# Splitting each accumulator right behind its last merge, ahead of the next superblock's input columns

## The chip, the cores and the metric

The kernel runs on one core of one Trainium2 chip. A core has five engines that run side by side, each with its own list of instructions that it works through in the written order: TensorE (PE, matrix products into PSUM banks), VectorE (DVE), ScalarE (ACT), GpSimd (POOL) and SyncE (SP, which here only starts transfers). ACT starts transfers as well. Engines wait for each other through semaphores. The metric is the device time of one execution in microseconds (us); lower is better.

## The reference

One layer of a decoder with three branches in parallel, on 2048 tokens of 1024 channels:

```python
h = rms_norm(x, norm_g[l])
p = h @ w_in[l]                       # 1024 -> 7552, split into the branches' inputs
y_a = rwkv7_mix(...) * silu(z_a)      # delta-rule recurrence, 512 channels
y_b = sliding_window_sink_attn(...) * silu(z_b)
y_c = memory_cross_attn(...) * silu(z_c)
gates = sigmoid(p_gate).reshape(bsz, t, 3, 1024)
merged = (gates[:, :, 0] * (y_a @ w_proj_a[l]) + gates[:, :, 1] * (y_b @ w_proj_b[l])
          + gates[:, :, 2] * (y_c @ w_proj_c[l]))
x = x + merged @ w_out[l]
```

All inputs and outputs are float32.

## The kernel before

The tokens are worked through in four *superblocks* `sb` = 0 to 3 of 512 tokens. Activations lie transposed: channels on the 128 partitions, tokens along the row. Dense products keep float32 accuracy by splitting each operand into a high part (rounded to the format fp32r, a copy on ACT) and a low part (the rest, a subtraction on DVE); each product is then three matmuls, high by high, high by low and low by high, into one PSUM bank (`gemm3`, lines 430 to 432, and the same three in `output`, lines 1137 to 1139).

A weight is fetched by `wblock` as a 128x512 piece. In superblock 0 the raw piece is loaded by SP (line 411, tile `raw`, three buffers), its high part is made by ACT (line 412), its low part by DVE (line 413), and both are stored to DRAM by SP (line 416). The later superblocks load both parts ready made (line 408), with no work on ACT or DVE. The split pieces `whl` have eight buffers.

A superblock ends in a tail with these pieces:

- `merge(0, ...)`, the last of three merges into the eight accumulators `accs` (tiles `mB`, one for each block of 128 output channels, called block 0 to block 7 here). For each block PE runs 12 matmuls into a bank `mm` (two buffers), DVE multiplies the bank by the gate (line 1119, which frees the bank) and adds the product to the accumulator (line 1120). So PE can start block o only when line 1119 of block o - 2 is done.
- `x_cols(sb + 1, rb)`, the normalised input `hH`/`hL` of the next superblock: for each of eight column blocks a load of the transposed `x` on ACT's queue (line 1181), a multiplication on DVE (line 1182), the high part on ACT (line 1184) and the low part on DVE (line 1185). The last superblock has none.
- `output(sb, accs)`: first each accumulator is split into a high part (`a`, a tile `g2`, line 1126 on ACT) and a low part (`b`, a tile `mB`, line 1128 on DVE). There are nine `mB` buffers for eight accumulators, so a low part takes the buffer that the split before it freed. Then two halves n = 0, 1 of 512 output columns: for each block k a piece of `w_out`, and 12 matmuls into four banks (two `mm`, two `as_`), 192 in all. At the end of a half, `x` is loaded (ACT queue), added by DVE (line 1144, which frees the bank) and stored (ACT queue).

The order of the instructions on each engine isn't the order of the Python code. `order` collects all instructions, `lay_out` plays them through with estimated costs, and the resulting list of each engine is fixed. At each step it takes, among the instructions of an engine that are ready, the one with the lowest *rank*. The rank is the place in the program (line `s.rank = len(out)`), with a few corrections: readers of PSUM off PE, such as line 1119, come 600 places earlier, and weight pieces up to 1000 places earlier:

```python
        s.rank = len(out)
        if any(r[0].startswith("whl") and (s.bytes or r[5] == F32R) for r in s.writes):
            s.rank = max(s.rank - ahead, min(s.rank, 15))
        if s.eng != "PE" and any(r[4] for r in s.reads):
            s.rank -= 600
```

So moving code in the program moves ranks, and through them the lists.

Of the kernel before, what the change touches and what calls it, by code (L numbers as in the profile page):

```python
# [9 lines left out]
F32 = mybir.dt.float32  # L10
F32R = mybir.dt.float32r
BF16 = mybir.dt.bfloat16
I32 = mybir.dt.int32
AF = mybir.ActivationFunctionType
ALU = mybir.AluOpType
# [4 lines left out]
TB = 512  # L20
# [265 lines left out]
def build(tc, A, nsb=4):  # L286
    nc = tc.nc
    es = ExitStack()
    V, S, G, PE = nc.vector, nc.scalar, nc.gpsimd, nc.tensor

    def pool(name, bufs, **kw):
        return es.enter_context(tc.tile_pool(name=name, bufs=bufs, **kw))
# [7 lines left out]
    mp = pool("mp", 9)  # L300
# [5 lines left out]
    def g2(dt=F32, shape=(128, TB)):  # L306
        return gp_.tile(list(shape), dt, name="g2")
# [3 lines left out]
    def mm_ps():  # L311
        return ps.tile([128, 512], F32, name="mm", bufs=2)
# [4 lines left out]
    def s_ps():  # L317
        return ps.tile([128, 512], F32, name="as_", bufs=2)
# [41 lines left out]
    def pcol(name, i=0):  # L360
        o, w = PV[name]
        return pv[:, o + i:o + i + 1]
# [13 lines left out]
    def dcol(name, i=0):  # L376
        return dv[:, DV[name][0] + i:DV[name][0] + i + 1]
# [27 lines left out]
    def wblock(src, key=None):  # L405
        w = wp.tile([128, 2, 512], F32R, name="whl")
        if key in kept:
            nc.sync.dma_start(w.bitcast(F32), kept[key])
            return w[:, 0], w[:, 1]
        raw = wp.tile([128, 512], F32, name="raw", bufs=RAW)  # L410
        nc.sync.dma_start(raw, src)
        S.activation(w[:, 0], raw, AF.Copy)  # L412
        V.tensor_tensor(w[:, 1], raw, w[:, 0].bitcast(F32), op=ALU.subtract)  # L413
        if key is not None and nsb > 1:
            kept[key] = dp.tile([128, 2, 512], F32, name=f"k{len(kept)}")
            nc.sync.dma_start(kept[key], w.bitcast(F32))
        return w[:, 0], w[:, 1]
# [8 lines left out]
    def gemm3(out, pairs):  # L426

        n = len(pairs)
        for i, ((lh, ll), (rh, rl)) in enumerate(pairs):
            PE.matmul(out, lh, rh, start=i == 0, stop=False)  # L430
            PE.matmul(out, lh, rl, start=False, stop=False)  # L431
            PE.matmul(out, ll, rh, start=False, stop=i == n - 1)  # L432
# [30 lines left out]
    def proj(blk, hT, n=TB):  # L463
        o = mm_ps()
        gemm3(o[:, :n], [(w, (hT[0][:, k, :n], hT[1][:, k, :n])) for k, w in enumerate(wtiles(A["w_in"][blk], 8, ("in", blk)))])
        return o
# [166 lines left out]
    def shift(o, blk, mu, omu, sb, tag, bufs=1):  # L633
        t = rp.tile([128, TB], F32, name=tag, bufs=bufs)
        S.activation(t, o, AF.Copy, scale=omu)
        V.scalar_tensor_tensor(t[:, 1:], o[:, :TB - 1], mu, t[:, 1:], op0=ALU.mult, op1=ALU.add)
        V.scalar_tensor_tensor(t[:, 0:1], carry[sb % 2][:, blk:blk + 1], mu, t[:, 0:1], op0=ALU.mult, op1=ALU.add)
        V.tensor_copy(carry[1 - sb % 2][:, blk:blk + 1], o[:, TB - 1:TB])
        return t
# [461 lines left out]
    def gate(i, o, hT):  # L1101
        gp = proj(B_G + 8 * i + o, hT)
        t = gp_.tile([128, TB], F32, name="gt", bufs=2) if i else g2()
        S.activation(t, gp, AF.Tanh, scale=0.5)  # L1104
        return t

    def merge(i, yh, yl, accs, hT, first=False, orange=range(8), gates=None):
        for o in orange:
            yield 3.718
            w = [t.rearrange("p (k c) -> p k c", k=4) for t in wblock(A["w_proj"][i, o], ("proj", i, o))]  # L1110
            g = gates[o] if gates else gate(i, o, hT)
            pp = mm_ps()
            gemm3(pp, [((w[0][:, k], w[1][:, k]), (yh[k], yl[k])) for k in range(4)])
            if first:
                acc = mp.tile([128, TB], F32, name="mB")
                V.scalar_tensor_tensor(acc, g, 1.0, pp, op0=ALU.add, op1=ALU.mult)
                accs.append(acc)
            else:
                V.scalar_tensor_tensor(g, g, 1.0, pp, op0=ALU.add, op1=ALU.mult)  # L1119
                V.tensor_tensor(accs[o], accs[o], g, op=ALU.add)  # L1120

    def output(sb, accs):
        mh, ml = [], []
        for o in range(8):
            a = g2(F32R)
            S.activation(a, accs[o], AF.Copy)
            b = mp.tile([128, TB], F32R, name="mB")
            V.tensor_tensor(b, accs[o], a.bitcast(F32), op=ALU.subtract)
            mh.append(a)
            ml.append(b)  # L1130
        for n in range(2):
            op = [mm_ps(), s_ps(), mm_ps(), s_ps()]
            for k in range(8):
                wh, wl = wblock(A["w_out"][n, k], ("out", n, k))
                for tt in range(4):
                    tk = slice(tt * 128, (tt + 1) * 128)
                    PE.matmul(op[tt], mh[k][:, tk], wh, start=k == 0, stop=False)  # L1137
                    PE.matmul(op[tt], mh[k][:, tk], wl, start=False, stop=False)  # L1138
                    PE.matmul(op[tt], ml[k][:, tk], wh, start=False, stop=k == 7)  # L1139
            for tt in range(4):  # L1140
                rows = slice(sb * TB + tt * 128, sb * TB + (tt + 1) * 128)
                xr = g2()
                nc.scalar.dma_start(xr, A["x"][rows, n * 512:(n + 1) * 512])
                V.scalar_tensor_tensor(xr, op[tt], 0.5, xr, op0=ALU.mult, op1=ALU.add)
                nc.scalar.dma_start(A["out"][rows, n * 512:(n + 1) * 512], xr)
# [7 lines left out]
    def x_norm(sb):  # L1153
        t = hT_tiles()
        norm_T(4, pcols("norm_g"), *t, x0)
        return t
# [32 lines left out]
    hT = x_norm(0)  # L1189
# [3 lines left out]
    for sb in range(nsb):  # L1193
        wa = proj(B_WA, hT)
        low = shift(wa, B_WA, pcol("mu_wa"), dcol("omu_wa"), sb, "rr_")
        S.activation(low[EV], low[EV], AF.Tanh)

        lwla = [rp.tile([128, TB], F32R, name=f"lwla{i}") for i in range(2)]
        for t, h, o in zip(lwla, (EV, OD), (OD, EV)):
            S.activation(t[h], low[h], AF.Copy)  # L1200
            V.tensor_tensor(t[o], low[h], t[h].bitcast(F32), op=ALU.subtract)
        yas = []
        ya, yb, yc_ = ([], []), ([], []), ([], [])
        accs = []

        def stream_r():
            n = 2
            for p0 in range(0, 4, n):
                group, Z = [], rp.tile([128, 2, 2, NC_, C], F32, name="Z")
                dk = xp.tile([128, 2, NC_], F32, name="dk", bufs=2)  # L1210
                Nc = rp.tile([128, 2, NC_, 32], F32, name="Nc")
                for p in range(p0, p0 + n):
                    yield from rwkv_prep(p, p - p0, Z, dk, Nc, sb, hT, lwla, group)
                yield from rwkv_inverse(group, Z, Nc)
                yield from rwkv_chain(group, Z, dk, hT, yas)
            while pend:
                pend.pop(0)()
            yield 0.412

        def stream_f():  # L1220
            for h in range(4):
                yield from cross_head(h, sb, hT, *yc_)
            if not sb:
                rope_tables(0)
            yield from swa_kv(sb, hT)
            yield 6.938
            for j in range(4):
                yield from weave(swa_pair(j, sb, hT, *yb), merge(2, *yc_, accs, hT, first=True, orange=(2 * j, 2 * j + 1)))
            yield from merge(1, *yb, accs, hT)
            for o in range(8):  # L1230
                gates.append(gate(0, o, hT))
                yield 5.908

        gates = []
        for _ in weave(*(paced(g, PACE[min(sb, 1)][i]) for i, g in enumerate((stream_r(), stream_f())))):
            pass
        for p in range(4):
            split_y(yas[p], *ya, "a", p, sb)
        rb = None
        if sb + 1 < nsb:  # L1240
            rope_tables(sb + 1)
            rb = x_scales(sb + 1)
        for _ in merge(0, *ya, accs, hT, gates=gates):
            pass
        if rb is not None:
            hT = x_cols(sb + 1, rb)
        output(sb, accs)
    order(tc, manual)
    es.close()


def paced(g, paces):

    for f, d in zip(paces, g):
        yield f * d
# [85 lines left out]
```

## Time and profile before

| | us |
|---|---|
| median of the runs of before | 2281.17 (2280.58, 2281.17, 2286.04) |
| time of the profiled execution | 2283.99 |
| its span, first to last instruction | 2282.2 |
| PE busy | 2241.2 (98%) |
| DVE busy | 1541.3 (68%) |
| ACT busy | 916.9 (40%) |
| mean granted PE clock | 0.995 of full speed |

Of one execution the profile gives for each instruction when it started, how long it took, and, in square brackets, how long its engine had been idle just before and what ended that idle time. A row of the timeline reads: start in us from the span's beginning, duration, engine, line of the code, operation, output tile <- input tiles, shapes, how many were merged into the row. Matmuls overlap: one starts about every 0.23 us though each is shown as 0.39 us long, so gaps on PE are read from start to start. A share of busy time is a mean over stages that differ, and the change touches only the four tails, so they are looked at one by one.

### The profile page before, as it was taken

What the parts mean: (1) busy time and instruction counts of PE and PEld (TensorE: products, weight loads), DVE (VectorE), ACT (ScalarE), POOL (GpSimd) and SP (SyncE); (2) the same over time, 40 slices, a digit from 0 to 9 for tenths busy, and PEclk for the clock granted to TensorE, in tenths of its full rate; (3) what the DMA queues carried; (4) which work ended last, traced back from release to release, by engine and by line L of the source; (5) the groups of instructions that cost most, each with busy time, mean ns of one, the idle gap of its engine ahead of it and who ended that gap; (6) DMA issues with size and microseconds to landing.
All of it is one profiled execution on the core that took longest, in us unless ns stands there. A gap on an engine that the chain in (4) does not pass through costs nothing.

```text
span 2282.2 us, 36933 instructions
## 1 busy us (share of the span) xinstructions
PE 2241.2 (98%) x13684; PEld 1814.2 (79%) x13684; DVE 1541.3 (68%) x3967; ACT 916.9 (40%) x2006; POOL 148.6 (7%) x209
## 2 busy tenths in 40 slices
PE   7999989999999999999999999999999999999999
PEld 6788778777788877878888877877888887777887
DVE  6799689775568777954427967884345795796312
ACT  5554564545244354433214344442222535434210
POOL 2000010000000010000001001000000001000000
PEclk9999999999999999999999999999999999999999
DMA  6767546679844443437774434445675444343655
GB/s 215 273 225 252 185 153 217 222 258 341 302 155 160 146 148 130 157 138 239 232 265 129 151 127 139 157 136 183 231 252 196 155 147 151 115 153 121 204 193 193
DMA packets 146226, 430.55 MB, mean 189 GB/s; under 512 B 16640, under 2 KB 21120, under 8 KB 146048
## 3 DMA queue, kind: packets, MB, share of 16 engines
q1 hardware_dynamic: 129920, 398.83, 52.1%
q10 hardware_dynamic: 16128, 29.37, 3.9%
q8 instruction: 109, 1.79, 0.3%
q14 instruction: 69, 0.57, 0.1%
HBM read 333.24 MB, written 94.90 MB: 188 GB/s over the span
## 4 chain that ended last, share of the span: by engine, by line
PE 70%; DVE 12%; ACT 3%; DMA 2%; issue 1%; POOL 0%; SPq 0%; ACTq 0%; DVEq 0%; POOLq 0%
PE mm L431 17%; PE mm L430 17%; PE mm L432 16%; PE rw L731 1%; DVE ibc L779 1%; PE mm L1139 1%; PE mm L1137 1%; PE mm L1138 1%; PE rw L852 1%; PE oo L1092 1%; DVE ibc L780 1%; PE oo L967 1%; PE rw L845 1%; DVE Yi L781 1%; PE rw L837 1%
## 5 line engine op out<-in xcount | busy, mean ns | idle before, releaser
L430 PE MATMUL mm<-hH,whl 128*128 128x512 f32 x1888 | 751.1, 398 | 4.6 <-DVE g L899 3.8
L431 PE MATMUL mm<-hL,whl 128*128 128x512 f32 x1888 | 752.4, 398 | 0.0
L432 PE MATMUL mm<-hH,whl 128*128 128x512 f32 x1888 | 747.4, 396 | 0.0
L430 PEld LDWEIGHTS mm<-hH,whl 128*128 128x128 f32 x1888 | 355.7, 188 | 76.7 <-DVE g L899 4.3
L431 PEld LDWEIGHTS mm<-hL,whl 128*128 128x128 f32 x1888 | 355.6, 188 | 71.1 <-issue 0.7
L432 PEld LDWEIGHTS mm<-hH,whl 128*128 128x128 f32 x1888 | 355.8, 188 | 68.6
L412 ACT ACTIVATE whl<-raw 128x512 fp32r<-128x512 f32 x178 | 111.7, 630 | 183.4 <-PE mm L432 79.6
L413 DVE TENSOR_TENSOR whl<-raw,whl 128x512 fp32r<-128x512 f32 x178 | 123.6, 696 | 65.7 <-ACT whl L412 64.6
L430 PE MATMUL mm<-yh,whl 128*128 128x512 f32 x384 | 152.8, 398 | 1.4 <-DVE g L1119 1.4
L431 PE MATMUL mm<-yl,whl 128*128 128x512 f32 x384 | 151.4, 394 | 0.0
L432 PE MATMUL mm<-yh,whl 128*128 128x512 f32 x384 | 151.3, 394 | 0.0
L843 ACT ACTIVATE SP<-Z,Pl 64x64 f32<-64x64 f32 x256 | 88.3, 345 | 118.7 <-DVE Z L853 114.9
L779 DVE STREAM_SHUFFLE ibc<-Nc 128x496 f32<-128x496 f32 (+30 forms) x248 | 113.2, 474 | 0.1
L1119 DVE SCALAR_TENSOR_TENSOR g<-g,mm 128x512 f32<-128x512 f32 x32 | 21.9, 686 | 127.5 <-PE mm L432 127.4
L780 DVE TENSOR_TENSOR ibc<-ibc,Yi 128x496 f32<-128x496 f32 (+30 forms) x248 | 104.7, 422 | 3.5
L781 DVE TENSOR_TENSOR Yi<-Yi,ibc 128x496 f32<-128x496 f32 (+30 forms) x248 | 103.6, 418 | 1.2
L853 DVE SCALAR_TENSOR_TENSOR Z<-rw,Pl,SP 64x64 f32<-64x64 f32 x224 | 63.5, 283 | 46.6 <-PE rw L852 42.9
L1104 ACT ACTIVATE gt<-mm 128x512 f32<-128x512 f32 x64 | 37.8, 591 | 129.3 <-PE mm L432 129.2
L430 PEld LDWEIGHTS mm<-yh,whl 128*128 128x128 f32 x384 | 72.1, 188 | 16.6 <-DVE g L1119 2.5
L432 PEld LDWEIGHTS mm<-yh,whl 128*128 128x128 f32 x384 | 72.1, 188 | 14.8
L1066 ACT ACTIVATE g<-g,mxs,st 128x256 f32<-128x256 f32 (+1 forms) x128 | 74.6, 584 | 22.8 <-DVE mxs L1059 22.5
L431 PEld LDWEIGHTS mm<-yl,whl 128*128 128x128 f32 x384 | 72.2, 188 | 13.9
(1882 smaller groups left out, 3789.6 us busy)
## 6 DMA issues: line engine op xcount, KB each, us to landing
whl<-k SPq DMA_DIRECT2D x486, 512.0 KB, 3.3
k<-whl SPq DMA_DIRECT2D x162, 512.0 KB, 3.2
raw<-in_w_in SPq DMA_DIRECT2D x118, 256.0 KB, 3.7
g<-in_x ACTq DMA_DIRECT2D x32, 256.0 KB, 5.0
out<-g ACTq DMA_DIRECT2D x32, 256.0 KB, 3.6
raw<-in_w_proj SPq DMA_DIRECT2D x24, 256.0 KB, 3.6
rt<-in_x ACTq DMA_DIRECT2D x24, 256.0 KB, 5.2
rt<-in_xt ACTq DMA_DIRECT2D x24, 256.0 KB, 5.5
```

The costliest lines, as they stand in the source:

```text
L412: S.activation(w[:, 0], raw, AF.Copy)
L413: V.tensor_tensor(w[:, 1], raw, w[:, 0].bitcast(F32), op=ALU.subtract)
L430: PE.matmul(out, lh, rh, start=i == 0, stop=False)
L431: PE.matmul(out, lh, rl, start=False, stop=False)
L432: PE.matmul(out, ll, rh, start=False, stop=i == n - 1)
L779: V.stream_shuffle(bc[:, :, :w], N_[:, :, s + 1:], [s] * 32)
L780: V.tensor_tensor(bc[:, :, :w], bc[:, :, :w], Y[:, :, s:s + 1].to_broadcast([128, n, w]), op=ALU.mult)
L781: V.tensor_tensor(Y[:, :, s + 1:], Y[:, :, s + 1:], bc[:, :, :w], op=ALU.add)
L843: S.activation(SP[h, i], Z[h, i, e, c], AF.Copy, scale=g[4][h, c:c + 1])
L853: upds = [V.scalar_tensor_tensor(Sst[h, g[0]] if c == NC_ - 1 else Z[h, i, e, c + 1], pS[h, i, e], g[4][h, c:c + 1], SP[h, i], op0=ALU.mul ...
L1066: S.activation(prs[b][:, i, m0:], prs[b][:, i, m0:], AF.Exp, scale=r2[:, b, i:i + 1], bias=mx[:, b, i:i + 1], accum_out=mx[:, b, 2 + i:3 + i])
L1104: S.activation(t, gp, AF.Tanh, scale=0.5)
```

## The change

The loop that splits the accumulators leaves `output` and becomes a function `split_acc`. The last merge is called block by block, and behind each block its accumulator is split. `x_cols` comes behind all of that, and `output` receives the parts.

```diff
-    def output(sb, accs):
-        mh, ml = [], []
-        for o in range(8):
-            a = g2(F32R)
-            S.activation(a, accs[o], AF.Copy)
-            b = mp.tile([128, TB], F32R, name="mB")
-            V.tensor_tensor(b, accs[o], a.bitcast(F32), op=ALU.subtract)
-            mh.append(a)
-            ml.append(b)
+    def split_acc(acc):
+        a = g2(F32R)
+        S.activation(a, acc, AF.Copy)
+        b = mp.tile([128, TB], F32R, name="mB")
+        V.tensor_tensor(b, acc, a.bitcast(F32), op=ALU.subtract)
+        return a, b
+
+    def output(sb, mh, ml):
         for n in range(2):
             op = [mm_ps(), s_ps(), mm_ps(), s_ps()]
...
-        for _ in merge(0, *ya, accs, hT, gates=gates):
-            pass
+        parts = []
+        for o in range(8):
+            for _ in merge(0, *ya, accs, hT, gates=gates, orange=(o,)):
+                pass
+            parts.append(split_acc(accs[o]))
         if rb is not None:
             hT = x_cols(sb + 1, rb)
-        output(sb, accs)
+        output(sb, *zip(*parts))
```

No instruction is added or removed and none changes its shape. The lists of SP and POOL stay the same; those of PE, DVE and ACT change in the tails of superblocks 0, 1 and 2 alone. In superblock 3, which has no `x_cols`, all lists stay as they were. The line numbers behind the change are lower by one from `output`'s matmuls on (1136 to 1138 for 1137 to 1139, 1143 for 1144, 1181 and 1184 for 1182 and 1185), and the split is at 1124 (ACT, before 1126) and 1126 (DVE, before 1128).

The first place is DVE in superblock 0, from block 3 of the last merge (gate tile `g_5749`) to block 5 (`g_5831`; block 4 is `g_5790`). Before:

```order
L1119 SCALAR_TENSOR_TENSOR g_5749<-g_5749,mm 128x512
L1182 TENSOR_TENSOR rt<-rt 128x512
L1120 TENSOR_TENSOR mB<-mB,g_5749 128x512
L1185 SCALAR_TENSOR_TENSOR hL<-rt,c_pv,hH 128x512
L1119 SCALAR_TENSOR_TENSOR g_5790<-g_5790,mm 128x512
L413 TENSOR_TENSOR whl<-raw,whl 128x512
L1120 TENSOR_TENSOR mB<-mB,g_5790 128x512
L1185 SCALAR_TENSOR_TENSOR hL<-rt,c_pv,hH 128x512
L413 TENSOR_TENSOR whl<-raw,whl 128x512
L1119 SCALAR_TENSOR_TENSOR g_5831<-g_5831,mm 128x512
```

And now the same stretch (`g_6077` and `g_6103` are the high parts of blocks 2 and 3):

```order
L1119 SCALAR_TENSOR_TENSOR g_5749<-g_5749,mm 128x512
L1181 TENSOR_TENSOR rt<-rt 128x512
L1126 TENSOR_TENSOR mB<-mB,g_6077 128x512
L1120 TENSOR_TENSOR mB<-mB,g_5749 128x512
L1184 SCALAR_TENSOR_TENSOR hL<-rt,c_pv,hH 128x512
L413 TENSOR_TENSOR whl<-raw,whl 128x512
L1119 SCALAR_TENSOR_TENSOR g_5790<-g_5790,mm 128x512
L1126 TENSOR_TENSOR mB<-mB,g_6103 128x512
L413 TENSOR_TENSOR whl<-raw,whl 128x512
L1119 SCALAR_TENSOR_TENSOR g_5831<-g_5831,mm 128x512
```

The splits of blocks 2 and 3 have come in, and a weight piece now stands ahead of block 4's line 1119 rather than behind it.

The second place is DVE in the same tail around the end of the last merge (block 7 has the gate `g_5913`). Before, from block 7's line 1119 to the second split, that of block 1 (`g_6225`):

```order
L1119 SCALAR_TENSOR_TENSOR g_5913<-g_5913,mm 128x512
L413 TENSOR_TENSOR whl<-raw,whl 128x512
L1120 TENSOR_TENSOR mB<-mB,g_5913 128x512
L1185 SCALAR_TENSOR_TENSOR hL<-rt,c_pv,hH 128x512
L1182 TENSOR_TENSOR rt<-rt 128x512 x2
L413 TENSOR_TENSOR whl<-raw,whl 128x512
L1182 TENSOR_TENSOR rt<-rt 128x512
L1185 SCALAR_TENSOR_TENSOR hL<-rt,c_pv,hH 128x512 x2
L413 TENSOR_TENSOR whl<-raw,whl 128x512
L1185 SCALAR_TENSOR_TENSOR hL<-rt,c_pv,hH 128x512
L1128 TENSOR_TENSOR mB<-mB,g_6225 128x512
```

Now, from block 6's addition to the last split (`g_6181` and `g_6207` are the high parts of blocks 6 and 7):

```order
L1120 TENSOR_TENSOR mB<-mB,g_5872 128x512
L1181 TENSOR_TENSOR rt<-rt 128x512
L413 TENSOR_TENSOR whl<-raw,whl 128x512
L1119 SCALAR_TENSOR_TENSOR g_5913<-g_5913,mm 128x512
L1126 TENSOR_TENSOR mB<-mB,g_6181 128x512
L1120 TENSOR_TENSOR mB<-mB,g_5913 128x512
L413 TENSOR_TENSOR whl<-raw,whl 128x512
L1184 SCALAR_TENSOR_TENSOR hL<-rt,c_pv,hH 128x512
L1126 TENSOR_TENSOR mB<-mB,g_6207 128x512
```

Block 1's split stood behind eleven instructions that followed block 7's line 1119; now block 7's own split stands behind four, and here too a weight piece stands ahead of line 1119. On PE one matmul of `output` (block 0 into the first `as_` bank) moves up ahead of the merge's block 6, and in half n = 1 the fourth bank is first written behind 53 matmuls of that half instead of 40.

The third place is DVE in superblock 1, blocks 2 to 4 of the last merge (gates `g_11048`, `g_11079`, `g_11110`). Before:

```order
L1119 SCALAR_TENSOR_TENSOR g_11048<-g_11048,mm 128x512
L1182 TENSOR_TENSOR rt<-rt 128x512
L1120 TENSOR_TENSOR mB<-mB,g_11048 128x512
L1182 TENSOR_TENSOR rt<-rt 128x512
L1119 SCALAR_TENSOR_TENSOR g_11079<-g_11079,mm 128x512
L1185 SCALAR_TENSOR_TENSOR hL<-rt,c_pv,hH 128x512
L1120 TENSOR_TENSOR mB<-mB,g_11079 128x512
L1185 SCALAR_TENSOR_TENSOR hL<-rt,c_pv,hH 128x512
L1119 SCALAR_TENSOR_TENSOR g_11110<-g_11110,mm 128x512
```

Now:

```order
L1119 SCALAR_TENSOR_TENSOR g_11048<-g_11048,mm 128x512
L1126 TENSOR_TENSOR mB<-mB,g_11331 128x512
L1120 TENSOR_TENSOR mB<-mB,g_11048 128x512
L1181 TENSOR_TENSOR rt<-rt 128x512
L1119 SCALAR_TENSOR_TENSOR g_11079<-g_11079,mm 128x512
L1126 TENSOR_TENSOR mB<-mB,g_11352 128x512
L1120 TENSOR_TENSOR mB<-mB,g_11079 128x512
L1184 SCALAR_TENSOR_TENSOR hL<-rt,c_pv,hH 128x512
L1119 SCALAR_TENSOR_TENSOR g_11110<-g_11110,mm 128x512
```

A split has taken the place of a piece of `x_cols` in each block; the number of instructions between two line 1119 is the same.

## The prediction

> **What bounds the kernel now.** I read the page first, for the busy shares and the chain of work that ended last.
>
> ```profile
> PE 2241.2 (98%) x13684; PEld 1814.2 (79%) x13684; DVE 1541.3 (68%) x3967; ACT 916.9 (40%) x2006; POOL 148.6 (7%) x209
> PE 70%; DVE 12%; ACT 3%; DMA 2%; issue 1%; POOL 0%; SPq 0%; ACTq 0%; DVEq 0%; POOLq 0%
> ```
>
> PE works nearly all the time and carries the chain. A change that adds and removes nothing can therefore gain only what PE waits, and lose only by new waits of PE. So the view of PE's waits comes next (who waits <- for whom: total us, times, longest):
>
> ```profile
> PE rw L456 <- DVE g L451: 10.3, 1, 10.3
> PE mm L1139 <- DVE mB L1128: 4.2, 1, 4.2
> PE mm L430 <- DVE g L1119: 1.4, 1, 1.4
> PE as__11638 L1137 <- DVE g L1144: 0.8, 1, 0.8
> PE as__16808 L1137 <- DVE g L1144: 0.6, 1, 0.6
> ```
>
> The first is the start of the kernel. The second is a wait for the low part of an accumulator, the very instruction that moves; it happens once, so in one tail only. The third is a wait in the last merge of superblock 0, the last two lie inside `output` of superblocks 1 and 2. The windows from `output`'s first matmul to the next superblock's first one, for superblocks 0, 1 and 2, then two windows inside the first (start:end, length, busy us and count of PE, PEld, DVE, ACT, POOL, granted PE clock, DMA share, GB/s):
>
> ```profile
> 577.44:628.52 51.08, 46.83 (x193) 37.83 (x192) 22.97 (x36) 10.50 (x17) 0.00 (x0) 0.93 0.86 315
> 1134.31:1179.06 44.75, 43.92 (x193) 35.81 (x192) 12.28 (x19) 1.73 (x3) 0.00 (x0) 1.00 0.76 259
> 1684.75:1729.15 44.40, 43.81 (x194) 35.97 (x192) 11.80 (x18) 1.24 (x3) 0.00 (x0) 1.00 0.77 260
> 582.00:586.72 4.72, 0.54 (x3) 0.11 (x1) 4.72 (x9) 2.86 (x5) 0.00 (x0) 0.89 0.90 313
> 586.72:592.43 5.71, 5.71 (x13) 4.45 (x14) 4.69 (x8) 0.63 (x1) 0.00 (x0) 0.50 0.94 338
> ```
>
> The same 192 matmuls take 51.08 us in superblock 0 and 44.75 and 44.40 in the next two. In the fourth row PE stands while DVE is busy all of the 4.72 us; in the fifth PE runs, but at half its clock: 13 matmuls in 5.71 us. PE's timeline shows both edges:
>
> ```profile
> 577.44 0.39 PE L1137 MATMUL mm<-whl,g 128*128 128x512 f32 x1
> 582.15 0.39 PE L1138 MATMUL as__6256<-whl,g 128*128 128x512 f32 x1
> 586.72 0.79 PE L1139 MATMUL mm<-whl,mB 128*128 128x512 f32 x1 [4.18 <-DVE mB L1128]
> 592.43 0.43 PE L1137 MATMUL as__6256<-whl,g 128*128 128x512 f32 x1
> ```
>
> **What the change takes away.** DVE's rows for the tail of superblock 0, and two of PE's, in the last merge:
>
> ```profile
> 565.65 0.68 DVE L1119 SCALAR_TENSOR_TENSOR g<-g,mm 128x512 f32<-128x512 f32 x1
> 566.25 0.75 DVE L1185 SCALAR_TENSOR_TENSOR hL<-rt,c_pv,hH 128x512 fp32r<-128x512 f32 x1
> 566.91 0.69 DVE L1120 TENSOR_TENSOR mB<-mB,g 128x512 f32<-128x512 f32 x1
> 568.12 0.68 DVE L1119 SCALAR_TENSOR_TENSOR g<-g,mm 128x512 f32<-128x512 f32 x1
> 570.58 0.68 DVE L1119 SCALAR_TENSOR_TENSOR g<-g,mm 128x512 f32<-128x512 f32 x1
> 585.97 0.70 DVE L1128 TENSOR_TENSOR mB<-mB,g 128x512 fp32r<-128x512 f32 x1
> ...
> 566.39 0.50 PE L430 MATMUL mm<-yh,whl 128*128 128x512 f32 x1 [1.38 <-DVE g L1119]
> 572.00 0.39 PE L430 MATMUL mm<-yh,whl 128*128 128x512 f32 x1
> ```
>
> A step on DVE is 0.60 us (565.65 to 566.25), 0.66 behind line 1185 (566.25 to 566.91), as long as nothing is waited for. The wait of 4.18 ends with block 1's split, done at 586.67, which had its turn only behind `x_cols` and weight pieces. Now it stands ahead of block 2's addition. Only superblock 0 splits weights on ACT and DVE, and only there is DVE so far behind.
>
> The price of one `output` matmul comes from superblock 1: 44.75 less its wait of 0.99 (0.83 idle and the lost overlap) is 43.76 for 192, or 0.228. Superblock 0's 51.08 hold 7.3 us more than that: 582.15 to 586.72 is 4.57, less a step 4.34; then 13 matmuls in 5.71 rather than 2.96, 2.75; the rest are restarts.
>
> **What the new order costs.** Up to block 2's line 1119 (565.65) DVE's list is unchanged, so the 1.38 at PE's 566.39 stays. From there ten instructions, two of them the former line 1185, lead to block 4's line 1119: 565.65 + 8 x 0.60 + 2 x 0.66 = 571.77, 1.2 later than the 570.58 of before, done at 572.45. PE's block 6 needs it, began at 572.00, and would begin at 572.5 (PE followed DVE by 0.06 at 566.39). The `output` matmul that was moved ahead of it fills 0.23 of that; a restart costs 0.1 (0.50 long, not 0.39). So `output` starts at 578.05 instead of 577.44 with 191 matmuls left: 578.05 + 191 x 0.228 = 621.6, against 628.52. **Sum: 6.9 us less.**
>
> The other lines 1119 by the same steps: block 5's, three on, is done at 574.2 and needed at 575.3; block 6's, eight on, done at 577.3, needed at 578.05; block 7's, thirteen on, starts at 579.6 and is done at 580.25, and PE wants its bank 12 matmuls into `output`, at 580.8. That margin, 0.5, is the thinnest. The splits are ahead of need from then on: the last, block 7's, starts at 582.7 and is wanted after seven blocks of 12 matmuls, at 597.
>
> What is pushed back instead is `x_cols`. Ten of its sixteen DVE instructions, mixed with four weight pieces, then follow to about 592, on ACT the high parts with them; PE needs `hH` at 621.6. That cover is 30 us, and its loads on ACT's queue share it. Weight pieces are made ten or more us ahead of use, so a shift by an instruction or two is hidden there too. In half 1 PE's fourth bank waits for a chain on ACT's queue: a bank added and stored, its buffer loaded again, added.
>
> ```profile
> g<-in_x ACTq DMA_DIRECT2D x32, 256.0 KB, 5.0
> out<-g ACTq DMA_DIRECT2D x32, 256.0 KB, 3.6
> ```
>
> Store and load make 8.6, and 0.7 for the addition 9.3. The chain is queued behind two weight pieces now, but PE asks after 53 matmuls, 12.1 us, instead of 40, 9.1. In superblocks 1 and 2 its place doesn't move, so their 0.8 and 0.6 stay. In their merges a split replaces a piece of `x_cols` one for one:
>
> ```profile
> 1123.58 0.69 DVE L1120 TENSOR_TENSOR mB<-mB,g 128x512 f32<-128x512 f32 x1
> 1124.33 0.61 ACT L1126 ACTIVATE g<-mB 128x512 fp32r<-128x512 f32 x1
> 1124.78 0.69 DVE L1119 SCALAR_TENSOR_TENSOR g<-g,mm 128x512 f32<-128x512 f32 x1
> 1126.15 0.39 PE L430 MATMUL mm<-yh,whl 128*128 128x512 f32 x1
> ```
>
> Block 3's line 1119 stays at 1124.78, done at 1125.47, and PE's block 5 wants it at 1126.15. The next split needs ACT's high part, ready at 1124.94, and DVE gets there at 1125.38. Cost: nothing, or 0.1 either way.
>
> The profiled execution took 2283.99, 2.8 above the median of 2281.17; the sum is made against it (2277.1) and I carry the saving over to the median: **2274.3 us**.
>
> **Is the half clock part of every execution?** Windows of 3.41 us around three of the drops:
>
> ```profile
> 298.94:302.35 3.41, 1.31 (x9) 0.87 (x8) 3.33 (x8) 3.39 (x13) 0.00 (x0) 1.00 0.97 335
> 302.35:305.77 3.41, 1.68 (x4) 1.40 (x5) 3.29 (x8) 2.51 (x8) 1.54 (x1) 0.50 0.69 246
> 312.59:316.01 3.41, 1.45 (x8) 0.78 (x7) 3.34 (x6) 0.79 (x2) 0.00 (x0) 1.00 0.40 128
> 316.01:319.42 3.41, 3.41 (x19) 2.79 (x19) 2.96 (x8) 0.62 (x2) 0.00 (x0) 0.50 0.67 220
> 582.25:585.66 3.41, 0.29 (x2) 0.00 (x0) 3.41 (x7) 2.62 (x5) 0.00 (x0) 1.00 0.93 346
> ```
>
> The clock fell behind windows in which PE was still busy 1.31 and 1.45 of 3.41 us. A wait of 4.18 leaves at least one such window however the windows lie: if it straddles two evenly, 2.09 of one, 61%, is idle. So I take the half clock as part of nearly every execution before. The Trainium skill, page "TensorE: Matmul & The Clock Gate", section "What's actually happening", says that the clock falls only after an idle window of about 3.4 us and that the windows run freely; by that a wait of 4.18 would hold a whole one in (4.18 - 3.41) / 3.41, 23% of executions. By the skill the median lost 4.3 rather than 7.1 in the wait, the saving is 6.9 - 2.75 = 4.15, and the time 2277.0. The trace contradicts that page: its drops followed windows that were not idle.
>
> **Rivals.**
> 1. *No half clock in the executions behind the median* (the mechanism just told, whatever its rule): 2281.17 - 4.15 = 2277.0. For it: 2.8 us between the profiled execution and the median is just the price of one such spell. Against it: the windows above.
> 2. *A weight piece takes the place of the split.* Block 7's line 1119 now stands behind a weight piece, and that behind a transfer:
>
> ```profile
> 554.91 9.37 DMA raw<-in_w_out
> ...
> 572.31 0.39 SPq L411 DMA_DIRECT2D raw<-in_w_out  x1
> ...
> 578.30 0.63 ACT L412 ACTIVATE whl<-raw 128x512 fp32r<-128x512 f32 x1 [2.09 <-DMA raw<-in_w_out]
> ```
>
> Its transfer was issued at 572.31 and landed some 6.0 us later, when ACT ran the high part at 578.30; DVE reaches the piece at 579.0, just in time. If it takes the 9.37 of the first row, DVE stands 3.4 more and PE 2.9: saving 4.0, time 2277.2. Against it: it takes a longer landing than this execution's.
> 3. *Slower.* In the merges of superblocks 1 and 2 each split stands ahead of the next line 1119 of DVE, and waits for ACT, whose list also starts `x_cols`' loads. If ACT holds the high part back by more than 0.44 (1125.38 - 1124.94) plus the 0.68 that PE has to spare (1126.15 - 1125.47), PE waits in every block. To end 6.8 above before, PE would have to lose 13.7 us in these two tails, nearly 1 us in each of their 16 blocks: ACT late by 2.0 each time. Time from 2288 on; half of it gives back the gain. Against it: ACT began the high part at 1124.33, 0.06 after the addition was done (1123.58 + 0.69).
> 4. *It does nothing*: excluded for superblock 0 as the split is no longer behind `x_cols`; PE can't wait for it there.
>
> **How the numbers follow.** The forecast has 0.78, rival 1 0.07, rival 2 0.06, rival 3 0.09 (0.08 of it slower than the bound, the rest within). 0.3% of 2281, 6.8 us, is about what a measurement of this kernel can tell from no change, and the sum of 6.9 lies right on it: of the forecast's 0.78 I put 0.48 beyond and 0.30 inside. Faster 0.48, within 0.44, slower 0.08. The runs of before spread over 5.5 us, so the range reaches 3.8 below the forecast, and above it past rivals 1 and 2 (2277) with half that spread more, 2280.0; the forecast's own range is 2271.5 to 2277.5.
>
> **What would show it.** In the profile behind the change: no wait of PE for the split's low part; `output` of superblock 0 about 44 us long at full clock; the 1.4 wait for line 1119 still there; PE's block 6 some 0.5 later; `x_cols` ending near 592, 30 us ahead of use; 0.8 and 0.6 unchanged. A PE wait for line 1119 over 1.5 us in any tail, or a window at half clock there, makes the prediction wrong.

## The result and the profile after

The changed kernel took 2274.45 us (median of six executions, 2271.17 to 2276.13) against 2282.58 for six of the kernel before (the three known ahead of the prediction are among them). The ratio is 0.9959 with a 95% interval of 0.9946 to 0.9972, that is 9.4 us less, 6.4 to 12.3. The forecast was 2274.3, 6.9 us less. Later comparisons, told below, put the ratio at 0.9974 (0.9965 to 0.9983) and 0.9971 (0.9961 to 0.9982), so the first one lies high: in the later groups of runs, 105 executions of the kernel before have a mean of 2282.15 and 18 of the changed one a mean of 2275.94, 6.2 us less.

The profiled execution of the changed kernel took 2271.17 us, its span is 2269.3. Busy shares and the chain of work that ended last, from its page, read as before (PE 98%, and PE carries the chain):

```profile
PE 2234.6 (98%) x13684; PEld 1809.9 (80%) x13684; DVE 1539.4 (68%) x3967; ACT 918.0 (40%) x2006; POOL 148.4 (7%) x209
PE 73%; DVE 12%; ACT 2%; issue 1%; DMA 0%; POOL 0%; DVEq 0%; ACTq 0%; POOLq 0%
```

In the view of PE's waits of the changed kernel only one line of the tails is left, the wait of 0.6 in superblock 2, now 0.5 (the first two lines below lie outside the tails). The 4.2 for the split's low part is gone, and so are the 1.4 for line 1119 and the 0.8 in superblock 1:

```profile
PE rw L456 <- DVE g L451: 10.2, 1, 10.2
PE mm L430 <- DVE g L899: 3.8, 1, 3.8
PE as__16808 L1136 <- DVE g L1143: 0.5, 1, 0.5
```

The windows of the changed kernel: the last merge of superblock 0, then `output` of superblocks 0, 1 and 2 (columns as in the prediction):

```profile
552.18:574.31 22.13, 22.13 (x101) 18.30 (x99) 19.14 (x32) 10.82 (x18) 0.00 (x0) 1.00 0.95 348
574.31:617.60 43.29, 43.29 (x192) 35.85 (x191) 21.38 (x34) 10.73 (x18) 0.00 (x0) 1.00 0.89 317
1123.37:1167.07 43.70, 43.70 (x194) 35.96 (x193) 11.81 (x19) 3.30 (x5) 0.00 (x0) 1.00 0.80 266
1672.64:1717.02 44.38, 43.90 (x194) 35.88 (x192) 11.72 (x19) 3.30 (x5) 0.00 (x0) 1.00 0.79 263
```

And the window of the last merge in the kernel before:

```profile
553.47:577.44 23.97, 22.54 (x99) 17.95 (x98) 18.25 (x30) 11.08 (x19) 0.00 (x0) 1.00 0.90 302
```

`output` of superblock 0 runs without a gap and at full clock: 43.29 us for 51.08. Between the two profiled executions the span shrank by 12.9 us (2282.2 to 2269.3), twice the 6.2 us, so most readings of this pair need care:

| stretch | before | after | difference |
|---|---|---|---|
| start to the last merge of superblock 0 | 553.47 | 552.18 | -1.3 |
| last merge of superblock 0 | 23.97 | 22.13 | -1.8 |
| `output` of superblock 0 | 51.08 | 43.29 | -7.8 |
| `output` of superblock 1 | 44.75 | 43.70 | -1.05 |
| all the rest | | | -0.9 |

The first row can't be the change: no instruction up to there has another place. The second and the fourth are what the prediction said would stay. DVE's rows in the changed kernel show why the last merge has no wait here, and, in the last row, block 1's split, which had run at 585.97:

```profile
559.79 0.68 DVE L413 TENSOR_TENSOR whl<-raw,whl 128x512 fp32r<-128x512 f32 x1
560.68 0.69 DVE L1119 SCALAR_TENSOR_TENSOR g<-g,mm 128x512 f32<-128x512 f32 x1 [0.20 <-PE mm L432]
...
561.95 0.69 DVE L1126 TENSOR_TENSOR mB<-mB,g 128x512 fp32r<-128x512 f32 x1
```

In the profile of before the weight piece ahead of block 2's line 1119 stood at 565.05, held up by its transfer, and PE waited for DVE; here it starts at 559.79 and DVE waits for PE (0.20). Whether the change does that, or the execution, is the first question for the experiments. The second is how much of the 7.8 is the wait, and how much the half clock behind it.

### The profile page after: what moved, and what is told of

It reads as the page before. It is cut to its first block, busy times and chain, and to the rows that moved or that the text cites. A ratio compares the mean times of both kernels' runs of the same rounds, so it can differ in the third digit from the quotient of the medians.

```text
span 2269.3 us, 36925 instructions
## 1 busy us (share of the span) xinstructions
PE 2234.6 (98%) x13684; PEld 1809.9 (80%) x13684; DVE 1539.4 (68%) x3967; ACT 918.0 (40%) x2006; POOL 148.4 (7%) x209
## 4 chain that ended last, share of the span: by engine, by line
PE 73%; DVE 12%; ACT 2%; issue 1%; DMA 0%; POOL 0%; DVEq 0%; ACTq 0%; POOLq 0%
PE mm L431 18%; PE mm L430 18%; PE mm L432 17%; PE mm L1136 1%; PE mm L1138 1%; PE mm L1137 1%; PE rw L731 1%; DVE ibc L779 1%; PE rw L852 1%; PE rw L845 1%; DVE ibc L780 1%; PE oo L967 1%; PE oo L1092 1%; PE rw L837 1%; DVE Yi L781 1%
```

## The experiments

Twelve runs, in three groups of four; each group ran on one chip, beside runs of the kernel before. The theory was: DVE's queue makes the wait, the idle PE brings the half clock, and all of the gain lies in superblock 0. The rivals: no half clock in most executions; a share of the gain in superblocks 1 and 2; the place right behind each merge being what matters.

### Both kernels again

> The kernel before, unchanged, for a second profile. Theory (a wait of 4 us for block 1's split in superblock 0 and a spell at half clock behind it belong to nearly every execution): ratio 1.000 within 0.1%, a wait for the split of 3 to 5 us, a granted clock of 0.5 behind it, output of superblock 0 at 51 us. Rival (no half clock in most executions): output at 48.3. Open: the wait of 1.4 us for line 1119 in the last merge of superblock 0 hung on a weight transfer of 9.4 us in the first profile; if that is a matter of the single execution it is smaller or gone here, and so may be the 0.8 in superblock 1.

> The changed kernel, unchanged, for a second profile. Theory: 2274.4 us, 2271 to 2276, 8 us below before; output of superblock 0 at 43.3 to 44 us, no wait for a split. The first profile showed neither the wait of 1.4 in the last merge of superblock 0 nor the 0.8 in superblock 1. If the change takes them away, they are missing again; if they are a matter of the single execution, one of the two comes back at 0.5 to 1.5 us.

The kernel before gave a ratio of 1.0005 (0.9995 to 1.0015), the changed one 0.9974 (0.9965 to 0.9983), median 2276.34. First the waits of PE and the window of `output` in superblock 0 in the second profile of the kernel before:

```profile
PE mm L1139 <- DVE mB L1128: 4.3, 1, 4.3
PE mm L430 <- DVE g L1119: 2.1, 3, 1.3
PE as__16808 L1137 <- DVE g L1144: 1.8, 1, 1.8
...
577.79:629.14 51.35, 46.97 (x193) 37.95 (x192) 23.07 (x36) 10.50 (x17) 0.00 (x0) 0.93 0.87 311
```

And in the second profile of the changed kernel:

```profile
PE as__16808 L1136 <- DVE g L1143: 1.1, 1, 1.1
PE mm L430 <- DVE g L1119: 0.9, 2, 0.8
...
553.50:577.46 23.96, 23.02 (x101) 18.05 (x98) 18.81 (x31) 9.97 (x17) 0.00 (x0) 1.00 0.89 315
577.46:620.75 43.29, 43.29 (x192) 35.85 (x191) 22.00 (x35) 11.24 (x18) 0.00 (x0) 1.00 0.91 328
```

The wait for the split and `output`'s length repeat to a few tenths in this profile. The wait for line 1119 is back in the changed kernel, and the last merge takes 23.96 there, as before. The wait of 0.8 in superblock 1 is absent from the kernel before this time, while superblock 2 waits 1.8. These small waits belong to the execution.

### One superblock or the others

```diff
+            if sb == 0:        # sb0_only;  sb12_only has: if sb > 0
                 parts.append(split_acc(accs[o]))
         if rb is not None:
             hT = x_cols(sb + 1, rb)
+        for o in range(len(parts), 8):
+            parts.append(split_acc(accs[o]))
```

> The split moved in superblock 0 alone; in superblocks 1 to 3 the lists are those of before. Theory (all of the gain lies in superblock 0): 2274.4 us, within 1.5 of the whole change. Rival (superblocks 1 and 2 give a part): 1 to 2 us above the whole change, with waits of 0.8 and 0.6 in the output of superblocks 1 and 2.

> The split moved in superblocks 1 and 2 alone; the list of superblock 0 is that of before. Theory: as before, 2281 to 2284 us, with the wait for the split of 3 to 5 us, the half clock behind it and output of superblock 0 at 51 us. Rival (superblocks 1 and 2 give a part): 1 to 2 us below before.

Superblock 0 alone gave 0.9972 (0.9961 to 0.9983), the same as the whole change on the same chip; superblocks 1 and 2 alone 1.0000 (0.9991 to 1.0009). The windows of the last merge and `output` in superblock 0 with the change in superblocks 1 and 2 alone:

```profile
552.34:578.59 26.25, 24.07 (x99) 19.02 (x98) 19.48 (x32) 11.70 (x20) 0.00 (x0) 0.93 0.89 307
578.59:628.13 49.54, 45.44 (x193) 37.09 (x192) 22.43 (x35) 10.50 (x17) 0.00 (x0) 0.97 0.88 320
```

So the gain lies in superblock 0; a share of up to 2 us in the others stays within the intervals. The 49.54 is a third value for the old order: its clock was at half for less of the time (0.97 against 0.93).

### Another way to the same order of things

Two kernels take only the queue ahead of block 1's split away. One keeps the splits together behind the whole merge, one leaves them in `output` and moves the columns behind it.

```diff
+        for _ in merge(0, *ya, accs, hT, gates=gates):     # split_then_cols
+            pass
+        parts = [split_acc(accs[o]) for o in range(8)]
         if rb is not None:
             hT = x_cols(sb + 1, rb)
```

```diff
-        if rb is not None:                                  # cols_last, from the kernel before
-            hT = x_cols(sb + 1, rb)
         output(sb, accs)
+        if rb is not None:
+            hT = x_cols(sb + 1, rb)
```

> The splits stand behind the whole last merge, but still ahead of the next superblock's input columns: only the place against the columns changes against before. The lists differ from the changed kernel's in superblock 0 alone. Theory (the wait came from the columns and weight pieces queued on DVE ahead of block 1's split): all of the gain, 2274.4 within 1.5 us. Rival (it takes a split right behind each block's merge): a wait of 1 to 3 us for a split stays, 2276 to 2281.

> The splits stay inside output, and the input columns move behind output in the program instead. Theory (DVE's queue ahead of the split is the cause, and the columns have 30 us to spare): all of the gain, 2274.4 within 1.5 us, no wait for a split. Rival (the columns come too late): a wait of PE for hH or hL at the start of superblock 1, 2 or 3, and a time above 2276.

Ratios 0.9970 (0.9961 to 0.9979) and 0.9975 (0.9964 to 0.9985); no wait for a split, no wait for `hH` or `hL`. `output` of superblock 0 in the first and in the second:

```profile
577.85:621.56 43.71, 43.71 (x193) 35.97 (x192) 22.55 (x36) 11.45 (x18) 0.00 (x0) 1.00 0.93 329
```

```profile
574.70:618.22 43.52, 43.52 (x194) 36.05 (x193) 21.77 (x35) 10.69 (x18) 0.00 (x0) 1.00 0.91 328
```

So what counts is the split's place against the columns, not its place against the merges.

### Only two blocks

```diff
+            if o < 2:
                 parts.append(split_acc(accs[o]))
```

(the others follow behind the columns, as above)

> Only the splits of blocks 0 and 1 are moved behind their merge; those of blocks 2 to 7 stay behind the columns. Block 1's split no longer waits. Theory by the steps of DVE: the columns and four weight pieces, twenty instructions from the end of block 7's line 1119 at 579.2, end at about 591.5, and PE, which has 24 matmuls or 5.5 us from output's start, wants block 2's split at 583.5: a wait of 2 to 8 us moves from block 1 to block 2, and the time is 2278 to 2286. Rival (only block 1's place mattered): 2274.4, no wait for a split above 0.5.

Ratio 0.9992 (0.9982 to 1.0002), median 2280.68. PE's rows where it waits:

```profile
584.27 0.39 PE L1137 MATMUL as__6256<-whl,g 128*128 128x512 f32 x1
587.50 0.50 PE L1138 MATMUL mm<-whl,mB 128*128 128x512 f32 x1 [2.83 <-DVE mB L1126]
...
588.92 0.63 PE L1137 MATMUL mm<-whl,g 128*128 128x512 f32 x1
```

The wait went from block 1 to block 2, as expected, and ended at nearly the same place (587.50 for 586.72): DVE's queue is the cause, whichever split stands behind it. The reckoned place, 591.5, was too late: the split stood behind 11 instructions that followed block 7's line 1119, not twenty. The half clock follows this shorter wait too (matmuls shown as 0.63 us long instead of 0.39).

### What the half clock costs

Matmuls that repeat a product are put ahead of the waiting one in the kernel before, 14 or 7 of them:

```diff
                     PE.matmul(op[tt], mh[k][:, tk], wl, start=False, stop=False)
+                    if sb == 0 and n == 0 and k == 1 and tt == 0:
+                        for _ in range(14):                 # fill;  fill7 has 7
+                            PE.matmul(op[tt], mh[k][:, tk], wh, start=False, stop=False)
                     PE.matmul(op[tt], ml[k][:, tk], wh, start=False, stop=k == 7)
```

> The kernel before, with 14 matmuls more on PE right ahead of its wait for block 1's split in superblock 0; all other lists are unchanged. They repeat a product into the first bank, so 128 rows of the output hold that product 14 times too often. 14 x 0.227 = 3.2 us of work go into the wait of 4.2. Theory (the wait ends when DVE has done the split, and the half clock comes from the idle PE): the wait shrinks to about 1.0 us, the end of the wait stays, the half clock behind it is gone, and the kernel with more work is 2.75 us faster than before, near 2279.8. Rival 1 (no half clock in most executions): the same time as before within 0.5 us. If the fill pushes back something else, up to 3 us slower.

> As the kernel with 14 more matmuls ahead of the wait, but with 7: 1.6 us of work in the wait, so that it is left at about 2.6 us. The same output rows come out wrong by 7 products. Theory (an idle PE of 2 to 3 us is enough for the clock to fall, as behind the waits of 2.2 and 2.8 us of two other profiles): one window of 3.4 us at half clock behind the wait, 7 to 8 matmuls at twice their time, 1.7 us; the time is 1 us below before and 1 above the one with 14. Rival (the clock falls only when PE idles for a whole window of 3.4 us): full clock behind the wait, the same time as with 14, 2 us below before.

With 14: ratio 0.9991 (0.9982 to 1.0000), 2.0 us less with 3.2 us more work. Its wait, the window behind it, and `output`:

```profile
586.47 0.50 PE L1142 MATMUL mm<-whl,mB 128*128 128x512 f32 x1 [1.17 <-DVE mB L1128]
...
577.04:625.59 48.55, 47.32 (x207) 38.51 (x206) 23.07 (x36) 10.51 (x17) 0.00 (x0) 1.00 0.91 329
586.47:589.88 3.41, 3.41 (x15) 2.84 (x16) 2.81 (x5) 0.63 (x1) 0.00 (x0) 1.00 1.00 344
```

The wait ends where it ended before (586.47, 586.72), the clock stays full, and `output` is 2.5 us shorter than the 51.08. So in the profiles the half clock is a cost of its own. Over the executions it comes to 2.0 us, with an interval of 0 to 4.1, so the time alone leaves open that it is rare. The granted clock of the executions doesn't: its mean is 0.9965 over the 11 with 14 matmuls and 0.9957 over the 29 of the kernel before beside them, and 0.0008 of 2282 us is 1.8 us of full clock.

With 7: ratio 0.9996 (0.9988 to 1.0005), 0.9 us less, expected 1. Its wait, and the windows ahead of the clock's drop and behind it:

```profile
586.94 0.50 PE L1142 MATMUL mm<-whl,mB 128*128 128x512 f32 x1 [2.13 <-DVE mB L1128]
...
584.53:587.94 3.41, 1.28 (x6) 0.86 (x5) 3.41 (x6) 0.63 (x1) 0.00 (x0) 1.00 0.84 282
587.94:591.35 3.41, 3.41 (x9) 2.68 (x8) 2.12 (x4) 0.63 (x1) 0.00 (x0) 0.50 0.98 374
```

A wait of 2.13 us was enough for one window of half clock. The time alone doesn't separate this kernel from either rival; its profile does.

### The same means at another wait

```diff
+    zero = bp.tile([128, 128], F32R, name="zero")
+    S.activation(zero, ones1.to_broadcast([128, 128]), AF.Copy, scale=0.0)
...
             PE.matmul(out, lh, rl, start=False, stop=False)
+            if i == n - 1:
+                for _ in range(fill):          # 14 in one product of superblock 0, else 0
+                    PE.matmul(out, zero, rh, start=False, stop=False)
             PE.matmul(out, ll, rh, start=False, stop=i == n - 1)
```

The planner counts these matmuls as taking no time, so that it leaves the rest where it was.

> The changed kernel with 14 matmuls more on PE at another wait of superblock 0, that of 3.8 us behind 299 us for line 899, at which every profile so far shows the clock at half afterwards. They multiply by a tile of zeros, into the bank that is just being summed, so the output stays right; all other lists are unchanged but for one more ACT instruction at the start. Theory (the half clock comes from the idle PE and costs 0.2 us in each of 11 matmuls): no half clock between 302 and 308, 2.3 us below the changed kernel. Rival (the bank that is finished 3.2 us later holds up its readers): a new wait of 1 to 3 us behind it, and the time of the changed kernel or more.

> The changed kernel once more, beside the one with the zero matmuls, and a third profile. Theory: 6 to 7 us below before, output of superblock 0 at 43.3 us. The wait in the last merge is 0 if the weight pieces of that merge's start were loaded early (second w_out load issued 2 us or more ahead of the merge's start or at its start) and about 1 if they were late; the changed order has no say in it.

> The kernel before once more, a third profile. Theory: ratio 1.000, a wait for block 1's split of 3 to 5 us, output of superblock 0 at 49 to 51.5 us with one or two windows of 3.4 us at half clock behind the wait; a wait in the last merge of 0 or 1 to 2 us by the same rule as in the changed kernel. If a profile without any half clock behind the wait turns up, output is at 48.3.

The kernel before gave 0.9999 (0.9991 to 1.0008), the changed one 0.9971 (0.9961 to 0.9982), median 2274.44, and the one with the zero matmuls 0.9961 (0.9949 to 0.9973), median 2272.41 of five. The last two intervals overlap, so the 2 us between these kernels are not a shown gain. The profile with the zero matmuls, at the wait and behind it (last row: from one PE instruction ahead of the wait to one behind it):

```profile
298.33 3.36 PE L436 MATMUL mm<-hH,zero 128*128 128x512 f32 x14
301.95 0.63 ACT L414 ACTIVATE whl<-raw 128x512 fp32r<-128x512 f32 x1 [2.19 <-PE mm L437]
302.60 0.60 ACT L909 ACTIVATE g<-mm 128x512 f32<-128x512 f32 x1
304.27 0.50 PE L432 MATMUL mm<-hH,whl 128*128 128x512 f32 x1 [2.36 <-DVE g L910]
...
304.27:307.68 3.41, 3.41 (x15) 2.84 (x16) 3.35 (x6) 1.74 (x7) 1.97 (x1) 1.00 0.67 214
297.20:320.51 23.31, 17.68 (x93) 13.68 (x93) 21.08 (x44) 10.25 (x27) 1.97 (x1) 0.93 0.49 165
```

The same places in the third profile of the changed kernel:

```profile
299.94 0.60 ACT L898 ACTIVATE g<-mm 128x512 f32<-128x512 f32 x1
302.21 0.80 PE L430 MATMUL mm<-hH,whl 128*128 128x512 f32 x1 [3.85 <-DVE g L899]
...
302.21:307.80 5.59, 5.59 (x13) 4.48 (x14) 5.38 (x8) 0.84 (x5) 1.97 (x1) 0.50 0.40 130
296.84:319.71 22.87, 17.04 (x80) 13.03 (x79) 20.98 (x44) 10.25 (x27) 1.97 (x1) 0.78 0.49 168
```

The half clock is gone: 15 matmuls in 3.41 us for 13 in 5.59. But the wait shrank by 1.5 only, not by 3.2. ACT had to wait 2.19 us for the longer product before it made the next weight piece and read the bank (302.60 for 299.94), and DVE's instruction that PE waits for (line 899, now 910) came later with it. Behind it PE waits 0.78 us more for DVE where there was no wait, and 1.62 for 1.11. From one PE instruction ahead of the wait (line 472, now 481) to one behind it (line 746, now 757) it takes 23.31 us, within the 22.45 to 23.93 of the 13 other profiles and not below the 22.87 beside it. So at this place the rival is right: what the full clock gave, the later end of the product took back. Where the lower time of this kernel comes from, if it is one, stays open.

### The wait in the last merge

The expectation for the third profiles named a rule: the wait for line 1119 depends on how late the weight pieces are when the last merge begins. The second load of `w_out` (its issue on SP), less the start of that merge, against the wait, over all profiles but that of the zero matmuls:

| kernel | second `w_out` load less merge start, us | waits for line 1119 in all, us |
|---|---|---|
| cols_last | -0.4 | 0 |
| after | -0.3 | 0 |
| sb0_only | 0.5 | 0 |
| after_again | 1.0 | 0.94 |
| fill | 1.4 | 1.27 |
| before | 1.4 | 1.38 |
| before_again | 1.6 | 1.56 |
| split_then_cols | 1.9 | 1.91 |
| after_third | 2.0 | 1.54 |
| two_blocks | 2.5 | 1.39 |
| before_third | 2.7 | 1.94 |
| fill7 | 2.9 | 2.22 |
| sb12_only | 3.3 | 2.18 |

Two of these loads on SP, of the changed kernel and of the one with the change in superblocks 1 and 2:

```profile
551.90 0.50 SPq L411 DMA_DIRECT2D raw<-in_w_out  x1
```

```profile
555.68 0.44 SPq L411 DMA_DIRECT2D raw<-in_w_out  x1
```

All these loads were issued by 556.80, ahead of the first instruction with a new place (block 1's split, at 561.95 in the first profile of the changed kernel and later in the others). So the lateness can't come from the change, and the wait follows it in both orders (the third profile of the changed kernel, at 1.54, waits longer than the expected 1). That it has nothing to do with the order at all is not shown: the three earliest cases all have the splits ahead of the columns.

## Why the prediction was right

The time came out 0.15 us from the forecast, which is luck within the spread; the saving was 9.4 in that comparison and 6.2 in the later groups, around the 6.9. The mechanism is what the runs bear out.

- *The wait of 4.18 and its cause.* Right: 4.10 to 4.28 in all four profiles with the old order in superblock 0, gone in all seven in which that queue no longer stands ahead of it, moved to block 2 when only two splits were moved.
- *Only superblock 0.* Right (0.9972 alone, 1.0000 for the others).
- *The half clock, 2.75.* Mechanism right, size somewhat high. The clock was at half for 6.83 us in the first two profiles of the old order, with `output` at 51.08 and 51.35, and for 3.41 us in the other two, with 49.54 and, in the third profile of the kernel before, 49.94; the prediction read the longer case as every execution's. The run with 14 matmuls puts it near 2.0 on average. Rival 1 (no half clock, saving 4.15) would put the ratio at 0.9982. That lies outside the intervals of the first comparison and of the splits behind the whole merge (0.9972 and 0.9979 at most), but on the edge of the two later ones. What speaks against it besides is the half clock in every profile of the old order and the mean clock of the run with 14.
- *Output at 0.228 per matmul.* 43.29 for 191 is 0.227; the sum had 43.55.
- *PE's block 6 half a us later, `output` from 578.05.* Mis-sized: in the second profile of the changed kernel, whose weights were about as late as in the profile of before, PE waits only 0.17 there and `output` starts at 577.46, against 577.44. The merge and `output` together are 67.25 there against 75.05, 7.8 less rather than 6.9. What the half clock lacked and this term had too much nearly cancel: over the four profiles of the old order and three of the changed kernel, `output` went from 50.48 on average to 43.29, 7.2, of which 0.23 is the matmul that moved ahead.
- *The 1.4 wait stays, the 0.8 and 0.6 stay.* Wrong as a statement on the next profile, since it read one execution's lateness as fixed. The sum didn't rest on it. The sign of being wrong that the prediction had named, a wait for line 1119 over 1.5, didn't come: the 1.54 of the third profile are two waits, 0.84 and 0.70.
- *Rival 2 (a weight piece ahead of block 7's line 1119) and rival 3 (ACT holds up the splits in superblocks 1 and 2).* Neither came: no wait for line 1119 behind block 6 in any profile of the changed kernel, no slower superblock 1 or 2.
- *The columns' cover of 30 us.* Right: the last `hL` of the changed kernel starts at 587.25, and PE wants the first at 617.60.
- *The chances.* The saving lies on the bound of 0.3%, as the text said: 0.41% in the first comparison, 0.26 and 0.29 in the later ones.

## What to carry to other kernels

A short wait of the busiest engine can cost more than its length. Count what comes behind it, here about 2 us of slower matmuls for 4 of waiting, and look at the granted clock in windows right behind each wait. Where an engine works its queue in order, the cure is the place in the queue: work with 30 us to spare stood ahead of work that was needed at once, and each of three ways to turn them round gave the same gain. Work that filled a wait helped here only where nobody waited for that work: it kept the clock at both waits, but at the second it held up the chain that the wait hung on. And a wait that hangs on a transfer should be taken from several executions before it is called fixed.

## What had not been expected of the hardware

The clock fell for waits shorter than a window. Within a profile its drops lie whole multiples of 3.413 us apart (at 302.35, 316.01 and 585.66 in the first profile of before: 4 and 79 steps), so the trace has a grid of such windows. In the tail of superblock 0 it fell at each wait of 2.13 us or more that PE had (2.13, 2.18, 2.22, 2.83 and the four of about 4.2), for one or two windows, and at none of 1.94 or less. The row of the 2.18, from the run with the change in superblocks 1 and 2, and then the 1.94 with the window of its merge, from the third profile of the kernel before:

```profile
563.24 0.50 PE L430 MATMUL mm<-yh,whl 128*128 128x512 f32 x1 [2.18 <-DVE g L1119]
```

```profile
564.54 0.50 PE L430 MATMUL mm<-yh,whl 128*128 128x512 f32 x1 [1.94 <-DVE g L1119]
...
554.14:578.29 24.15, 22.21 (x100) 18.04 (x98) 18.65 (x31) 11.40 (x19) 0.00 (x0) 1.00 0.92 313
```

The first one's merge had a mean clock of 0.93 (its window is shown above), the second one's 1.00. It isn't a matter of length alone: with the zero matmuls the wait of 2.36 us at 304.27 was followed by full clock. It lay across two windows in which PE was busy for 64 and 67%. In the tail of superblock 0 the windows that ended with a drop had PE busy for 0 to 38%, and those at full clock that ended without one for 55% or more. That isn't the whole rule, for near 135 us, among smaller matmuls (128x1 and 128x256), the clock fell in most profiles at the end of a window with 73 or 74%. The grid also goes with the length of the slow spell. In the first profile of before the clock fell ahead of the end of the wait, and two slow windows followed; in the third it fell behind it (588.00, the wait ended at 587.51), and one followed:

```profile
585.66:592.49 6.83, 5.77 (x14) 4.51 (x15) 5.81 (x10) 0.63 (x1) 0.00 (x0) 0.50 0.93 321
```

```profile
588.00:591.41 3.41, 3.41 (x10) 2.64 (x9) 2.29 (x5) 0.63 (x1) 0.00 (x0) 0.50 1.05 366
```

The Trainium skill, page "TensorE: Matmul & The Clock Gate", section "What's actually happening", asks for an idle window of about 3.4 us; the window ahead of the drop in the run with 7 matmuls had PE busy for 1.28 of its 3.41 us, so the trace disagrees. And work that computes nothing can make a kernel faster: 14 more matmuls in a wait, 2.0 us less (0 to 4.1).
